# FFN2's operands formed in place from x, held as two half tiles from FFN1's end to FFN2's end

## The chip, the cores and the metric

The kernel runs on one core of a Trainium2 chip. The metric is the device time of one execution in microseconds (us), the median of the runs shown. Five engines work side by side: TensorE (PE), VectorE (DVE), ScalarE (ACT), GpSimd (POOL) and SyncE (SP), each with its own queue of instructions; SP and POOL, and here and there ACT, issue the transfers (DMA).

## The reference

One decoder layer on 1024 prompt tokens and 32 sample tokens (8 sequences of 4), with a width of 1024 and 2816 hidden units:

```python
h = _modulate(_rms(x, p["ffn1_norm"]), sh1, sc1)
x = x + 0.5 * g1[:, None, :] * _swiglu(h, p["ffn1_w_gate"], p["ffn1_w_up"], p["ffn1_w_down"])
h = _modulate(_rms(x, p["mix_norm"]), sh2, sc2)
m, new = _mixer(h, conv[l], hst[l], shift[l], wkv[l], p)
x = x + g2[:, None, :] * m
h = _modulate(_rms(x, p["ffn2_norm"]), sh3, sc3)
x = x + 0.5 * g3[:, None, :] * _swiglu(h, p["ffn2_w_gate"], p["ffn2_w_up"], p["ffn2_w_down"])
y = _rms(x, final_norm)
```

`_swiglu` is `(silu(h @ w_gate) * (h @ w_up)) @ w_down`. The mixer projects h, runs a gated linear recurrence (RG-LRU) on one half of the channels and a matrix-state recurrence (RWKV-7, here in 16 chunks of 64 tokens) on the other, and projects back with `w_out`. Shifts, scales and gates come from the conditioning input; the states of the samples are inputs and outputs.

## The kernel before

x is kept transposed: 128 partitions hold 8 blocks (k) of the 1024 channels, each with its tokens side by side, 1056 and 4 of padding (XW = 1060). The stages follow one another: FFN1 up, FFN1 down, mixer, FFN2 up, FFN2 down with the final norm.

Every matrix product runs as three passes (`mm3`, L61 to L63) over high and low parts. `split` makes the two parts of a weight or an operand: a copy on ACT (L46, tiles wh, fh) and a subtraction on DVE (L47, tiles wl, fl).

An FFN's up stage (`up_phase`) pairs token columns 0 to 527 (pair 0) with 528 to 1055 (pair 1). The hidden units come in 22 blocks; blocks 0 and 1 are plain products (tiles pg, pu), the others use fewer products of summed weights and summed operands (tiles pX, pY, pZ, pW, operands b and t1 to t4). For that `pair_rstd` makes the norm's factor of a pair (squares nt, sums nps by a matmul, factor rn, spread over the partitions as npb and nrs), `pair_unit` (L236) multiplies x by it, `Blocks.split` (L275, L276) makes the operands b and b2, `pair_scale` (L240) scales, and `sums` and `split_sums` make t1 to t4. In FFN2 the pairs are read from DRAM (dX, L1353) into tiles of their own, after the end of the mixer has stored x there (L1316).

The down stage (`down`) loads hidden rows back from DRAM (dh, L489), splits them, multiplies by the down weights into PSUM tiles pd, which rotate over seven buffers (`F`), and `acc_x` (L463, L466) adds each pd to x on DVE, the samples' part to sacc. The mixer's `w_out` does the same with tiles po. Its last part (`w_out_end`) is the third token piece (tokens 768 on) of the first half of the channels, in two output groups (og).

x is one tile. In FFN1 down it is loaded from the input by three transfers (L1481), in FFN2 down by four from dX (L1316). In between, the parts of x that lie in DRAM are scratch for the mixer (`Lg`, `LRO`). Pools (`opened`) place tiles in on-chip memory; a tile waits for those that held its place. The order of instructions on an engine is the scheduler's, by priorities and its own estimates of time, except under `in_order`, where it is the program's. Small constants of the recurrence (tiles spt, L578 to L592) are computed on DVE beside FFN1 down.

## Time and profile before

| what | value |
|---|---|
| median of 3 runs | 2209.8 us (2209.15 to 2214.6) |
| the profiled execution | 2204.8 us, span 2203.0 us |
| mean granted TensorE clock | 0.977 |
| PE / DVE / ACT / POOL busy | 95% / 64% / 34% / 10% |
| stages, by the timeline | FFN1 up to 562, FFN1 down to about 830, mixer to 1437, FFN2 up to 1922, FFN2 down to the end |

A row of the timeline gives the start and the length in us, the engine, the line, the operation, the tiles (output, then inputs), the shapes and how many instructions were put together; square brackets give the engine's idle time ahead of it and what ended that. In a table of windows, each engine has its busy us and in parentheses its instructions; PEclk is the share of full speed that TensorE's clock was granted.

### The profile page before, as it was taken

How to read it: one execution, taken by the hardware profiler on the slowest of the kernel's cores; microseconds unless marked ns; L12 is line 12 of the kernel's file. 1: busy time of each engine (PE TensorE's matmuls, PEld its weight loads, DVE VectorE, ACT ScalarE, POOL GpSimd, SP SyncE). 2: the span in 40 equal slices, each digit the busy share in tenths (PEclk: the TensorE clock that was granted, in tenths of full speed). 3: DMA queues.
4: the chain of work that ended last, by engine and by line, in shares of the span. 5: the costliest groups of instructions: out<-in, count | busy, mean ns of one | idle time of the engine just before them, and what ended most of it. 6: DMA issues, size and time to landing. Idle time of an engine off the chain costs nothing.

```text
span 2203.0 us, 41916 instructions
## 1 busy us (share of the span) xinstructions
PE 2098.9 (95%) x17209; PEld 1989.5 (90%) x17209; DVE 1409.2 (64%) x2954; ACT 743.2 (34%) x1289; POOL 209.4 (10%) x310
## 2 busy tenths in 40 slices
PE   6899999999999999999998899879999999999997
PEld 4899999999999998898886689879999999999997
DVE  5855555565865565775855775687666666585655
ACT  5633232333311135443342441264333333331213
...
PEclk8999999999999999999998999889999999999998
...
GB/s 253 88 152 144 140 148 140 136 148 90 251 107 73 84 67 65 87 117 163 122 177 157 190 173 143 140 125 69 83 75 77 83 79 73 123 205 74 109 37 79
DMA packets 148414, 266.80 MB, mean 121 GB/s; under 512 B 76272, under 2 KB 92800, under 8 KB 146176
## 3 DMA queue, kind: packets, MB, share of 16 engines
...
q8 instruction: 135, 2.21, 0.4%
q14 instruction: 55, 0.45, 0.1%
...
## 4 chain that ended last, share of the span: by engine, by line
PE 76%; DVE 10%; DMA 3%; issue 3%; ACT 3%; POOL 1%; SPq 1%; ACTq 0%; DVEq 0%; POOLq 0%
PE pd L61 7%; PE pd L62 7%; PE pd L63 7%; PE pX L61 4%; PE pZ L61 4%; PE pX L62 4%; PE pZ L63 4%; PE pX L63 4%; PE pW L61 4%; PE pW L63 4%; PE pW L62 4%; PE pZ L62 4%; PE pY L63 2%; PE pY L61 2%; PE pY L62 2%
## 5 line engine op out<-in xcount | busy, mean ns | idle before, releaser
L61 PE MATMUL pd<-fl,wh 128*128 128x384 f32 (+1 forms) x1056 | 340.9, 326 | 3.5 <-DVE fl L47 2.6
L63 PE MATMUL pd<-fh,wh 128*128 128x384 f32 (+1 forms) x1056 | 341.4, 324 | 0.0
L62 PE MATMUL pd<-fh,wl 128*128 128x384 f32 (+1 forms) x1056 | 341.4, 324 | 0.0
L46 ACT ACTIVATE wh<-wr 128x512 fp32r<-128x512 f32 (+1 forms) x254 | 192.1, 761 | 254.5 <-PE pZ L63 71.7
L47 DVE TENSOR_TENSOR wl<-wr,wh 128x512 fp32r<-128x512 f32 (+1 forms) x254 | 215.0, 851 | 89.8 <-ACT wh L46 84.3
L61 PEld LDWEIGHTS pd<-fl,wh 128*128 128x128 f32 x1056 | 198.9, 189 | 5.2 <-ACT wh L46 2.7
L62 PEld LDWEIGHTS pd<-fh,wl 128*128 128x128 f32 x1056 | 199.7, 189 | 0.0
L63 PEld LDWEIGHTS pd<-fh,wh 128*128 128x128 f32 x1056 | 199.4, 189 | 0.0
L61 PE MATMUL pW<-t,wh 128*128 128x266 f32 (+1 forms) x640 | 182.6, 285 | 0.0
L63 PE MATMUL pW<-t,wh 128*128 128x266 f32 (+1 forms) x640 | 182.3, 285 | 0.0
L62 PE MATMUL pW<-t,wl 128*128 128x266 f32 (+1 forms) x640 | 182.2, 285 | 0.0
L463 DVE SCALAR_TENSOR_TENSOR x<-pd,g3c,x 128x384 f32<-128x384 f32 (+1 forms) x192 | 107.0, 568 | 83.1 <-PE pd L63 83.1
L463 DVE SCALAR_TENSOR_TENSOR x<-pd,g1c,x 128x384 f32<-128x384 f32 (+1 forms) x192 | 107.4, 567 | 76.7 <-PE pd L63 76.6
L419 ACT ACTIVATE e<-e,bt 128x262 f32<-128x262 f32 x80 | 41.3, 516 | 293.8 <-DVE bt L418 274.2
L344 POOL DMA_DIRECT2D dh<-hf x88 | 48.0, 545 | 972.4 <-DVE hf L425 793.9
L46 ACT ACTIVATE fh<-wr 128x1056 fp32r<-128x1056 f32 x44 | 47.5, 1082 | 243.2 <-PE pd L63 193.7
L62 PEld LDWEIGHTS pW<-t,wl 128*128 128x128 f32 x640 | 120.8, 189 | 0.0
L61 PEld LDWEIGHTS pW<-t,wh 128*128 128x128 f32 x640 | 120.5, 188 | 0.0
L63 PEld LDWEIGHTS pW<-t,wh 128*128 128x128 f32 x640 | 120.5, 188 | 0.0
L47 DVE TENSOR_TENSOR wl<-s,wh 128x512 fp32r<-128x512 f32 x120 | 82.6, 689 | 55.3 <-ACT wh L46 55.2
L416 DVE TENSOR_TENSOR e<-pZ,e 128x266 f32<-128x266 f32 x80 | 34.4, 430 | 104.3 <-PE pZ L63 104.1
L46 ACT ACTIVATE wh<-s 128x512 fp32r<-128x512 f32 x120 | 75.4, 629 | 65.9 <-PE pW L63 31.4
(495 smaller groups left out, 5888.8 us busy)
## 6 DMA issues: line engine op xcount, KB each, us to landing
wa<-in_w_ada SPq DMA_DIRECT2D x72, 512.0 KB, 3.9
dh<-hf POOLq DMA_DIRECT2D x88, 264.0 KB, 2.3
...
wr<-in_ffn_w_gate SPq DMA_DIRECT2D x44, 512.0 KB, 3.5
wr<-in_ffn_w_up SPq DMA_DIRECT2D x44, 512.0 KB, 3.5
wr<-in_ffn_w_down SPq DMA_DIRECT2D x44, 512.0 KB, 4.2
ch<-dc ACTq DMA_DIRECT2D x32, 512.0 KB, 6.5
wr<-in_w_in SPq DMA_DIRECT2D x22, 512.0 KB, 3.9
```

Source lines behind the costliest of these rows:

```text
L46: nc.scalar.activation(hi, raw, AF.Copy)
L47: nc.vector.tensor_tensor(lo, raw, hi.bitcast(F32), op=ALU.subtract)
L61: nc.tensor.matmul(ps, wh, xl, start=(first and i == 0), stop=False, **kw)
L62: nc.tensor.matmul(ps, wl, xh, start=False, stop=False, **kw)
L63: nc.tensor.matmul(ps, wh, xh, start=False, stop=(last and i == n - 1), **kw)
L344: nc.gpsimd.dma_start(self.dH[m][:, 528 * p:528 * p + 528], hf)
L416: tt(g2, pz, u, op=ALU.add)
L419: nc.scalar.activation(g2[:, 0:n], g2[:, 0:n], AF.Silu, bias=bt[:, 0:1])
L463: nc.vector.scalar_tensor_tensor(x[:, ob, c:c + np_], ps[:, 0:np_], g[:, ob, 0:1], x[:, ob, c:c + np_], op0=ALU.mult, op1=ALU.add)
```

## The change

x becomes two tiles x0 and x1 (class `Halves`) of four channel blocks each, 4256 elements wide per partition (HW), in a pool that lives until the end. The second FFN's operands are views into them (`pair`): pair 0's and pair 1's loads into tiles of their own go, x is still stored to dX for the last addition, and a half's tile is allocated anew after FFN2 up (`x.new`) and read back from dX. The space of x0 serves as t2 and t4 of pair 0 (`t24`) once x0 has been used up, so x0 is read back later than x1. Every transfer, clearing and addition of x over all blocks becomes one per half (`HK`).

`w_out_end` goes; its place is taken by a block in which pair 0's norm factor and its eight `pair_unit` are made between the first product of output group 0 and the rest. In that block the raw weight tiles become three (one before) and the split ones three (four before). The mixer's scratch moves: the recurrence's (A to D) into x1, `Lg`'s six slots become three in each half, the samples' and the first gated output's into x0. In FFN2 up the pools are laid out anew, pair 1's norm sums start two blocks earlier in block 1, and a pool `gap` moves the hidden rows of FFN2 down's first groups to another place.

```diff
@@ -23,6 +23,7 @@
 
 XW = T + 4
 PAIRS = ((0, 264), (528, 266))
+HW = 4256
 SHC, NSH = T, T - (528 + 266)
 NORM_EPS = 1e-6
 GROUPS = [(0, 2), (2, 4)] + [(g, g + 3) for g in range(4, 22, 3)]
@@ -131,8 +132,30 @@
     eps = const.tile([128, 1], F32, name="eps")
     nc.vector.memset(eps, NORM_EPS)
 
+
+    class Halves:
+        def __init__(self, pool):
+            self.pool = pool
+            self.new()
+
+        def new(self):
+            self.t = [self.pool.tile([128, HW], F32, tag=f"x{i}", name=f"x{i}") for i in range(2)]
+            self.v = [t[:, 0:KD // 2 * XW].rearrange("p (k t) -> p k t", k=KD // 2) for t in self.t]
+
+        def __getitem__(self, at):
+            _, k, c = at
+            if isinstance(k, slice):
+                i = k.start // 4
+                return self.v[i][:, k.start - 4 * i:k.stop - 4 * i, c]
+            return self.v[k // 4][:, k % 4, c]
+
+
+        def pair(self, p, i):
+            return self.v[i][:, :, 528 * p:528 * p + 2 * PAIRS[p][1]].rearrange("p k (j t) -> p j k t", j=2)
+
+    HK = [slice(0, 4), slice(4, 8)]
     x = None
-    LRO = {"A": 4 * XW - 32, "B": 5 * XW, "C": 6 * XW, "D": 7 * XW}
+    LRO = {"A": 0, "B": 1084, "C": 2140, "D": 3196}
     mod = const.tile([128, 72, 9], F32, name="mod")
 
 
@@ -293,10 +319,13 @@
             for o, a, b in ((r(0, 0), r(0, 1), r(0, 0)), (r(0, 1), r(1, 1), r(0, 1)), (r(1, 1), r(1, 1), r(0, 0)), (r(1, 0), r(1, 0), r(1, 1))):
                 adder.tensor_tensor(o, a, b, op=ALU.subtract)
 
+
         def split_sums(self, tags):
-            for tag, (o, i, j) in zip(tags, (("t2", 1, 1), ("t1", 0, 0), ("t3", 0, 1), ("t4", 1, 0))):
+            for n, (o, i, j) in enumerate((("t1", 0, 0), ("t3", 0, 1), ("t2", 1, 1), ("t4", 1, 0))):
                 src = self.q(i, j)
-                self.o[o] = h, l = self.both(tag, o)
+                if n == len(tags) == 2:
+                    t = xp.tile([128, HW], F32R, tag="x0", name="t24")
+                self.o[o] = h, l = self.both(tags[n], o) if n < len(tags) else self.parts(t[:, 2128 * (n - 2):2128 * (n - 1)])
                 split(src, h, l)
 
     class Up:
...
@@ -1027,7 +1057,7 @@
             for p in range(2):
                 nc.tensor.transpose(pt[:, c, p].rearrange("p a t -> p (a t)"), yc[:, 4 * c + 2 * p:4 * c + 2 * p + 2].rearrange("p a b -> p (a b)"), ident)
         if "y" not in m:
-            gated(t0, 2 * CL, lambda j: pt[:, :, j // 2, j % 2, :], lambda sh, dt, n: x[:, 0:4, t0:t0 + 2 * CL] if n == "o1" else o(sh, dt, n), "q")
+            gated(t0, 2 * CL, lambda j: pt[:, :, j // 2, j % 2, :], lambda sh, dt, n: x[:, HK[0], t0:t0 + 2 * CL] if n == "o1" else o(sh, dt, n), "q")
             return
         o1 = gated(t0, 2 * CL, lambda j: pt[:, :, j // 2, j % 2, :], o, "q")
         ci = t0 // 384
@@ -1304,16 +1325,17 @@
     g1c = const.tile([128, KD, 9], F32, name="g1c")
     g3c = const.tile([128, KD, 9], F32, name="g3c")
     g2c = mod[:, 40:48, :]
-    rn3 = const.tile([128, 6], F32, name="rn3")
+    xp = None
     dX = [dram.tile([128, KD, 528], F32, name=f"dx{p}") for p in range(2)]
 
 
     def dx_move(queue, c, n, store, k0=0, k1=KD):
         for p in range(2):
             b, e = max(c, 528 * p), min(c + n, 528 * p + 528)
-            if e > b:
-                s, d = x[:, k0:k1, b:e], dX[p][:, k0:k1, b - 528 * p:e - 528 * p]
-                queue.dma_start(*((d, s) if store else (s, d)))
+            for h in HK:
+                if e > b and k0 < h.stop and h.start < k1:
+                    s, d = x[:, h, b:e], dX[p][:, h, b - 528 * p:e - 528 * p]
+                    queue.dma_start(*((d, s) if store else (s, d)))
 
     def norm_pool(ph):
         return opened(ph, "sp", {"t": 3, "sq": 2, "acc": 1, "rs": 2, "adar": 1, "rn": 2, "bt": 3}, side="right")
...
@@ -1344,13 +1367,16 @@
 
             def load_x(p):
                 w = PAIRS[p][1]
+                if rest is None:
+                    X[p] = [x.pair(p, i) for i in range(2)]
+                    return
                 X[p] = [slot(f"x{p}{i}", F32, f"x{p}{i}")[:, 0:8 * w].rearrange("p (j k t) -> p j k t", j=2, k=4) for i in range(2)]
                 for i in range(2):
                     for j in range(2):
                         n = min(w, 528 - w * j)
                         if n < w:
                             nc.gpsimd.memset(X[p][i][:, j, :, n:w], 0.0)
-                        (nc.sync if rest else nc.gpsimd).dma_start(X[p][i][:, j, :, 0:n], xsrc[p][:, 4 * i:4 * i + 4, w * j:w * j + n])
+                        nc.sync.dma_start(X[p][i][:, j, :, 0:n], xsrc[p][:, 4 * i:4 * i + 4, w * j:w * j + n])
 
             sn = [0, None]
 
@@ -1373,9 +1399,8 @@
                         for rs0 in r0:
                             pass
                     else:
-                        rs0 = spread(rn3, WU, spr)
                         W0 = up.plain(*R0)
-                    for k in range(KD):
+                    for k in range(KD) if rest else ():
                         pair_unit(X[0], 0, k, rs0)
                 if first:
                     first(sp, stage)
@@ -1398,9 +1423,9 @@
                     for k in range(KD):
                         next(late, None)
                         ps = up.plain_mm(W1, B[0], 0, k, k + 1, ps)
-                        if k == 1:
+                        if k == (1 if rest else 0):
                             next(r1)
-                        if k == 3:
+                        if k == (3 if rest else 1):
                             rs1 = next(r1)
                     for _ in late:
                         pass
@@ -1425,11 +1450,12 @@
                             up.plain_mm(W, B[1], 1, 0, KD, ps, js=(1,))
                         up.plain_out(u, ps, kept[:, T * u:T * u + T])
             B[1].sums(nc.vector)
-            B[1].split_sums(("e0", "e1", "c1", "x10"))
+            B[1].split_sums(("e1", "c1", "e0", "x10" if rest else "x00"))
         W = up.summed(*raws.pop(0))
         B[0].sums(nc.vector)
-        B[0].split_sums(("x11", "e2", "c0", "x00"))
-        wa = slot("x01", F32, "wa")
+        B[0].split_sums(("e2", "c0", "x11", "x00") if rest else ("e2", "c0"))
+        if rest:
+            wa = slot("x01", F32, "wa")
         bg = rest(sp, lambda k: wa[:, 1024 * (k % 2):1024 * (k % 2) + 1024]) if rest else iter(())
         with in_order(nc.tensor):
             for u in range(2, NH):
@@ -1469,8 +1495,8 @@
                  ("a10", "e0", "e1", "x10", "a11", "a12", "c1", "x01", "a00", "x11", "e2", "c0", "a01", "a02", "x00"), (), (),
                  first, lambda sp, stage: ada8(0, PY, sp, stage), rest)
     hp = None
-    xt = mx.enter_context(tc.tile_pool(name="xp", bufs=1, reuse_waits="tile")).tile([128, KD * XW], F32, tag="x", name="x")
-    x = xt.rearrange("p (k t) -> p k t", k=KD)
+    xp = es.enter_context(tc.tile_pool(name="xp", bufs=1, reuse_waits="tile"))
+    x = Halves(xp)
     with ExitStack() as ph:
         hid = opened(ph, "hid", {"fh": 3, "fl": 3}, side="right")
         sp = norm_pool(ph)
...
@@ -1478,7 +1504,8 @@
         early = ph.enter_context(ExitStack())
         more = Rows(early, "hidB", ("fh", "fl", "wh", "wl"), 3)
         for c, n in CH[::-1]:
-            nc.gpsimd.dma_start(x[:, :, c:c + n], xT[:, :, c:c + n])
+            for h in HK:
+                nc.gpsimd.dma_start(x[:, h, c:c + n], xT[:, h, c:c + n])
 
 
         def main_done():
@@ -1524,9 +1551,10 @@
 
         def Lg(name, n=T):
             ln[0] += 1
-            return xt[:, 1080 * (ln[0] % 6):1080 * (ln[0] % 6) + n]
-        wa = xt[:, 6480:6480 + T]
-        m["w2"] = xt[:, 7552:7552 + 512]
+            o = 1056 * (ln[0] % 3)
+            return x.t[ln[0] // 3 % 2][:, o:o + n]
+        wa = x.t[0][:, 3192:3192 + T]
+        m["w2"] = x.t[1][:, 3192:3192 + 512]
         nc.sync.dma_start(m["w2"], a["w2a2"])
         first = [Shifted(12), Shifted(4)]
         for j, *p in head:
...
@@ -1646,25 +1674,40 @@
         nc.sync.dma_start(a["hO"], m["hO"])
 
     with ExitStack() as ph:
-        PL_["w"] = PL_["wr"] = opened(ph, "wC", {"wr": 1, "wh": 4, "wl": 4})
-        tmp = opened(ph, "rC", {"nt": 1})
-        r3 = pair_rstd(0, lambda k: x[:, k, 0:528].rearrange("p (j t) -> p j t", j=2), lambda sh, name: P.tile(sh, F32, tag="wu", name=name),
-                       type("R", (), {"tile": staticmethod(lambda sh, dt, tag, name: rn3)}), tmp.tile([128, 2128], F32, "nt", "nt"))
-        for _ in range(2):
-            next(r3)
-        w_out_end()
+        PL_["w"] = PL_["wr"] = opened(ph, "wC", {"wr": 3, "wh": 3, "wl": 3})
+        nt = ph.enter_context(tc.tile_pool(name="rC", bufs=1, reuse_waits="tile")).tile([128, 2128], F32, tag="nt", name="nt")
+        rn = PL_["mc"].tile([128, 6], F32, name="rn3")
+        own = type("R", (), {"tile": staticmethod(lambda sh, dt, tag, name: rn if tag == "rn" else nt[:, 528:1056])})
+        W = [w_load(0, og) for og in range(2)]
+        r3 = pair_rstd(0, lambda k: x.pair(0, k // 4)[:, :, k % 4], lambda sh, name: P.tile(sh, F32, tag="wu", name=name), own, nt)
+        next(r3)
+        w0 = w_block(W[0], 0, 0, 2)
+        next(w0)
+        next(r3)
+        next(w0)
+        rs = next(r3)
+        for k in range(KD):
+            pair_unit([x.pair(0, i) for i in range(2)], 0, k, rs)
+        for w in (w0, w_block(W[1], 0, 1, 2)):
+            for _ in w:
+                pass
+        add_samples(g2c)
+        for i in range(2):
+            nc.gpsimd.memset(x.v[i][:, :, T:XW], 0.0)
+        dx_move(nc.gpsimd, 768, 288, True)
     mx.close()
     PL_["wn"] = T
     with ExitStack() as ph:
-        up_phase(ph, "ffn2", dX, sc3, 6, ("x10", "x11", "e2", "c1", "x00", "x01", "a10"), ("e0", "e1", "a11", "a12"), ("a00", "c0", "a01", "a02"))
+        up_phase(ph, "ffn2", None, sc3, 6, ("a00", "c0", "a01", "a02", "e2"), (), ("a10", "c1", "a11", "a12", "e0", "e1", "x00"))
+    x.new()
     PL_["wr"] = opened(es, "wrp", {"wr": 3}, side="right")
-    xt = es.enter_context(tc.tile_pool(name="xp", bufs=1, reuse_waits="tile")).tile([128, KD * XW], F32, tag="x", name="x")
-    x = xt.rearrange("p (k t) -> p k t", k=KD)
     with ExitStack() as ph:
         hid = opened(ph, "hid", {"fh": 3, "fl": 3}, side="right")
         sp = norm_pool(ph)
         PL_["w"] = opened(ph, "wp", {"wh": 3, "wl": 3}, side="right")
         early = ph.enter_context(ExitStack())
+
+        early.enter_context(tc.tile_pool(name="gap", bufs=1, reuse_waits="tile")).tile([128, 11000], F32, name="gap")
         more = Rows(early, "hidB", ("fh", "fl", "wh", "wl"), 3)
         for c, n in CH[::-1]:
             dx_move(nc.gpsimd, c, n, False)
```

The change moves instructions. In the rows below x_6357 is x0 and x_6358 is x1 of the first allocation, x_21289 and x_21290 those of the second; x_15572 is the tile of its own that pair 0 had before. Line numbers are those of each kernel (L492 is the add of `acc_x`, before L463; L48 the subtraction of `split`, before L47; L260 `pair_unit`, before L236).

DVE at the end of w_out, before:

```order
L463 SCALAR_TENSOR_TENSOR x<-po,mod,x 128x256
L466 TENSOR_TENSOR sacc<-po,sacc 128x32
L245 TENSOR_TENSOR shd<-mod 128x64
L472 TENSOR_TENSOR sacc<-sacc,mod 128x256
L473 TENSOR_TENSOR x<-x,sacc 128x8x32
L476 MEMSET sacc 128x256
L47 TENSOR_TENSOR wl<-wr,wh 128x512 x4
L236 TENSOR_TENSOR x_15572<-x_15572,nrs 128x2x264 x4
L276 SCALAR_TENSOR_TENSOR b_15631<-x_15572,sc_94,b_15631 128x264
```

and after:

```order
L48 TENSOR_TENSOR wl<-wr,wh 128x512 x2
L492 SCALAR_TENSOR_TENSOR x_6357<-po,mod,x_6357 128x256
L495 TENSOR_TENSOR sacc<-po,sacc 128x32
L260 TENSOR_TENSOR x_6357<-x_6357,nt 128x528 x4
L260 TENSOR_TENSOR x_6358<-x_6358,nt 128x528 x4
L492 SCALAR_TENSOR_TENSOR x_6357<-po,mod,x_6357 128x256
L495 TENSOR_TENSOR sacc<-po,sacc 128x32
L48 TENSOR_TENSOR wl<-wr,wh 128x1024
```

The splits of FFN2's first weights and the eight multiplications of pair 0 stood behind the last addition of w_out; now they stand ahead of the last five.

DVE at the start of FFN1 down, before:

```order
L463 SCALAR_TENSOR_TENSOR x<-pd,g1c,x 128x256
L466 TENSOR_TENSOR sacc<-pd,sacc 128x32
L463 SCALAR_TENSOR_TENSOR x<-pd,g1c,x 128x256
L466 TENSOR_TENSOR sacc<-pd,sacc 128x32
L581 TENSOR_TENSOR spt_8411<-spt_8410 128x4
L463 SCALAR_TENSOR_TENSOR x<-pd,g1c,x 128x384
L584 TENSOR_TENSOR spt_8412<-spt_8412,spt_8411 128x4
L463 SCALAR_TENSOR_TENSOR x<-pd,g1c,x 128x384
L585 TENSOR_SCALAR spt_8412<-spt_8412 128x4
```

and after:

```order
L614 TENSOR_TENSOR spt_8415<-spt_8415,spt_8414 128x4
L615 TENSOR_SCALAR spt_8415<-spt_8415 128x4
L616 TENSOR_TENSOR spt_8415<-spt_8415,spt_8413 128x4
L618 SCALAR_TENSOR_TENSOR spt_8416<-spt_8415,spt_8416 128x4
L621 TENSOR_SCALAR sp2c<-spt_8416 128x4
L622 TENSOR_SCALAR nsp_8448<-spt_8416 128x4
L492 SCALAR_TENSOR_TENSOR x_6357<-pd,g1c,x_6357 128x256
L495 TENSOR_TENSOR sacc<-pd,sacc 128x32
L492 SCALAR_TENSOR_TENSOR x_6357<-pd,g1c,x_6357 128x256
```

The small steps on spt stood between the additions, one at a time; now two additions (blocks 3 and 7) are followed by 19 of these steps in a row, of which the last six are shown, and then by the other additions.

POOL in FFN2, from the last store of hidden rows on, before:

```order
L344 DMA dh<-hf 128x528 x43
L1316 DMA x<-dx_99 128x8x288
L1316 DMA x<-dx_98 128x8x144
L1316 DMA x<-dx_99 128x8x240
L1316 DMA x<-dx_98 128x8x384
L344 DMA dh<-hf 128x528
```

and after:

```order
L373 DMA dh<-hf 128x528 x38
L1338 DMA x_21289<-dx_98 128x4x288
L373 DMA dh<-hf 128x528
L1338 DMA x_21289<-dx_97 128x4x144
L1338 DMA x_21289<-dx_98 128x4x240
L1338 DMA x_21289<-dx_97 128x4x384
```

Here only x0's four loads are left; x1's stand 38 stores earlier. The last store of hidden rows now stands behind one of x0's loads and ahead of three.

35 lines of the change are left out of this document (16 added, 19 removed).

## The prediction

> **What bounds the kernel now.** I began with the busy shares, the slices and the shares of the chain that ended last.
>
> ```profile
> PE 2098.9 (95%) x17209; PEld 1989.5 (90%) x17209; DVE 1409.2 (64%) x2954; ACT 743.2 (34%) x1289; POOL 209.4 (10%) x310
> PE   6899999999999999999998899879999999999997
> PEclk8999999999999999999998999889999999999998
> PE 76%; DVE 10%; DMA 3%; issue 3%; ACT 3%; POOL 1%; SPq 1%; ACTq 0%; DVEq 0%; POOLq 0%
> ```
>
> TensorE (PE) is the bound nearly everywhere; only its idle time and its half-clock time can be gained, and each new stall of it is lost in full. So the windows come next.
>
> ```profile
> 500.00:700.00 200.00, 200.00 (x1365) 198.83 (x1364) 131.79 (x287) 51.24 (x67) 5.95 (x9) 1.00 0.40 133
> 1000.00:1300.00 300.00, 276.31 (x3128) 237.37 (x3124) 195.64 (x453) 120.00 (x200) 63.34 (x99) 0.94 0.68 163
> 1430.00:1440.00 10.00, 7.67 (x60) 7.44 (x58) 5.70 (x18) 2.86 (x6) 0.49 (x1) 0.99 0.43 157
> 1440.00:1450.00 10.00, 5.12 (x23) 5.12 (x24) 10.00 (x20) 7.40 (x15) 3.46 (x7) 0.50 0.89 287
> 1460.00:1470.00 10.00, 6.27 (x45) 6.09 (x44) 6.12 (x11) 2.21 (x4) 0.00 (x0) 0.85 0.00 0
> 1470.00:1480.00 10.00, 8.78 (x70) 8.41 (x68) 7.47 (x19) 6.38 (x16) 0.00 (x0) 0.98 0.01 2
> 1480.00:1490.00 10.00, 8.06 (x57) 7.47 (x58) 8.99 (x26) 8.94 (x24) 0.00 (x0) 1.00 0.00 0
> 1490.00:1500.00 10.00, 6.83 (x56) 6.61 (x55) 10.00 (x14) 7.89 (x13) 0.00 (x0) 1.00 0.03 13
> 1900.00:2000.00 100.00, 96.55 (x630) 94.90 (x629) 66.15 (x130) 23.99 (x27) 5.20 (x7) 0.98 0.54 175
> ```
>
> The columns are the length, the busy us and counts of PE, PEld, DVE, ACT and POOL, then the granted clock. FFN1's passage from up to down (500 to 700) has no idle PE at all. Three places that the change touches have some: the end of w_out and the start of FFN2 (1430 to 1500, 2.33 + 4.88 + 10.06 us, and half clock in one window), FFN2's passage to down (3.45), and the mixer (23.7 in 1000 to 1300). What ends the idle stretches:
>
> ```profile
> 1435.89 0.49 DVE L463 SCALAR_TENSOR_TENSOR x<-po,mod,x 128x256 f32<-128x256 f32 x1 [1.02 <-PE po L63]
> 1437.71 0.48 DVE L463 SCALAR_TENSOR_TENSOR x<-po,mod,x 128x256 f32<-128x256 f32 x1 [1.24 <-PE po L63]
> 1439.52 2.42 DVE L47 TENSOR_TENSOR wl<-wr,wh 128x512 fp32r<-128x512 f32 x4
> 1441.87 2.56 DVE L236 TENSOR_TENSOR x<-x,nrs 128x528 f32<-128x528 f32 x4
> 1444.88 0.59 PE L61 MATMUL pg<-b,wh 128*128 128x264 f32 x1 [7.21 <-DVE b L276]
> 1446.18 0.77 POOL L1353 DMA_DIRECT2D x<-dx  x1 [5.81 <-ACT b L275]
> 1446.93 0.14 POOL L1352 MEMSET x<- 128x16 f32 x1
> 1465.75 1.07 PE L210 MATMUL nps<-ones,nt 128*88 128x1 f32 x12 [3.73 <-DVE nt L206]
> 1480.68 0.39 PE L61 MATMUL pg<-b,wh 128*128 128x266 f32 x1 [1.09 <-DVE b L276]
> 1482.77 4.24 ACT L240 ACTIVATE x<-x,sc 128x266 f32<-128x266 f32 x10
> 1499.26 0.39 PE L61 MATMUL pu<-b,wh 128*128 128x266 f32 x1 [3.17 <-ACT e L380]
> 1499.49 0.28 PE L62 MATMUL pu<-b,wl 128*128 128x266 f32 x1
> 1499.61 0.28 PE L63 MATMUL pu<-b,wh 128*128 128x266 f32 x1
> 1510.10 0.29 PE L61 MATMUL pX<-b,wh 128*128 128x266 f32 x1
> ```
>
> After the last add (1437.71) DVE splits unit 0's weights and scales pair 0 while PE stands 7.21 us; the loads of pair 1 are issued only at 1446, so its norm sums reach PE 3.73 us late; 3.17 us are lost to the gate's exponent on ACT. The first regular product starts at 1510.10.
>
> **The start of FFN2, in four terms.** (1) Unit 0's weight splits (2.42 us) and the eight scalings of pair 0 (2.56 for four, 5.12 in all) now stand in DVE's order before w_out's last adds; what remains between last product and unit 0 is the start of the splits of x, about 1.5 us by my count of the rows. But in w_out DVE then makes no add for 5.12 + 1.22 (one weight split of 128x1024, twice a 128x512 one: 2.42 / 4 x 2) = 6.3 us, and the PSUM tiles that PE may still fill cover some 2.3 of these (one add per 1.8 us, from 1435.89 to 1437.71, is PE's own rate here, and I count between one and two free tiles): a new stall of 4. Gain 7.21 - 1.5 - 4 = 1.7; ends -0.6 (nothing covered) and +5.7 (all covered). (2) At 1444.88 the gap is followed by half clock, so 5.12 busy us of that window did 2.56 us of work. The new gaps are shorter; I take half of it, 1.3, between 0 and 2.6. (3) Of the 10.06 idle us in 1460 to 1500 the wait for pair 1's loads goes, since no load is left, and its norm is taken a step earlier; the small waits for splits go with it. The exponent's stall stays and grows: ACT's ten scalings of 4.24 us now stand later, and some six of them (2.5) come ahead of it, 3.17 + 2.5 = 5.7. Gain 4.4, ends 0 and 6.9. (4) The clock of 0.85 in 1460 to 1470 becomes full: 0.15 x 6.27 = 0.9. Sum -8.3, ends +0.6 and -16. Pair 0's own loads lay beside w_out and save nothing more. At nothing I cost the memset (0.14 on POOL, once a half, and POOL waited 5.81 us ahead of its loads there), the samples' add in two halves (DVE is idle 4.3 us in 1430 to 1440) and the three raw weight tiles of w_out (their loads are ahead of their splits even now); without that cover they cost their own length, under 1 us together.
>
> **FFN1 up to down.** This term speaks against the change, and nothing in the change's purpose shows it.
>
> ```profile
> 548.22 2.67 POOL L1481 DMA_DIRECT2D x<-in_xT  x3 [9.22 <-ACT e L421]
> 563.02 0.47 DVE L463 SCALAR_TENSOR_TENSOR x<-pd,g1c,x 128x256 f32<-128x256 f32 x1
> 572.50 0.16 DVE L585 TENSOR_SCALAR spt<-spt 128x4 f32<-128x4 f32 x1
> 572.69 0.16 DVE L584 TENSOR_TENSOR spt<-spt,spt 128x4 f32<-128x4 f32 x1
> 1932.11 0.34 PE L61 MATMUL pd<-fl,wh 128*128 128x384 f32 x1
> 1932.28 0.34 PE L62 MATMUL pd<-fh,wl 128*128 128x384 f32 x1
> ```
>
> Before, three loads of x go out together, and each add waits for its own columns. A half tile is 4256 wide, no multiple of the 1060 of a block, so a load or add over several blocks counts as touching all between: the program's waits make the loads of one half follow each other's landing, and make every add to x0 but the fourth block's wait for all three. The order around it has turned: after the adds of blocks 3 and 7 stand 19 small steps of the mixer's constants (spt, each on the one before), and only then the next add. At 0.19 us (572.50 to 572.69) these are 3.6 us without an add. The first add starts at 563.02 as before; six spt steps (1.1) follow, and the second add, whose tile I put at 565.2, ends near 565.9. The third then starts at 569.5 and ends near 570.2 (0.47 and the samples' 0.2). PE has one tile left to fill (six matmuls of 0.17: 1.0 us, to 566.9) and stands 3.3 us. Three later waits in the same group, behind DVE's splits of the next group's operands, I count at 0.7 + 0.7 + 0.8. Sum +5.5. Nothing gives it back, as PE was never idle here. Ends: 0 (the PSUM tiles cover it) and +9 (half clock behind it too).
>
> **FFN2 up to down.**
>
> ```profile
> dh<-hf POOLq DMA_DIRECT2D x88, 264.0 KB, 2.3
> 1905.51 0.33 SPq L489 DMA_DIRECT2D wr<-dh  x1
> 1916.43 3.54 POOL L1316 DMA_DIRECT2D x<-dx  x4 [3.00 <-PE pZ L63]
> 1924.15 1.77 PE L61 MATMUL pd<-fl,wh 128*128 128x288 f32 x7 [2.56 <-DVE fl L47]
> 1925.72 0.44 PE L62 MATMUL pd<-fh,wl 128*128 128x288 f32 x1
> 1928.02 0.29 PE L62 MATMUL pd<-fh,wl 128*128 128x288 f32 x1
> ```
>
> Before, the hidden rows are loaded at 1905 and their split ends PE's wait of 2.56; then matmuls start 0.24 apart until 1928 instead of 0.13, which loses another 1.8; the rest of the 3.45 idle us is 0.9. Now the gap pool puts these rows where room comes free about a unit earlier, and a group of five matmuls moves even among the last products: 2.56 + 1.8 + 0.9 = 5.3 can go. Against it, x0 can be loaded only after PE's last reading of t24 (near 1922), in three steps, each behind the landing of the one before (2.5 to 3 us by the row at 1916.43, about 0.9 to issue, and 2.3 us to landing in the stores' row): complete near 1932, while x1 came long before. Four adds to x1 cover the first steps; then an add to x0 stands behind three splits, and I count PE waits of 2.0 + 0.6 + 0.9 = 3.5, with clock loss 0.8. Net -1.0; ends -5.3 and +3.
>
> **The mixer.** The recurrence's scratch now shares x1, the gated output and the sample's scratch share x0; counts of instructions are the same. Its loads of x from DRAM are eight, as before. I take 0, from -3 to the third rival's price.
>
> **Sum.** The profiled execution is 2204.8 us, 1.8 of them outside the span of 2203.0, and 5.0 under the median of 2209.8 of the runs shown. -8.3 + 5.5 - 1.0 + 0 = -3.8: 2201.0 on the profile's scale, 2206 as a median. 0.3% of 2209.8 is 6.6 us, about what a measurement can tell from no change.
>
> **Rivals.** First, the stalls are covered. If PSUM's tiles carry PE over the spt steps (0) and over the scalings (5.7), and the other terms reach their good ends (2.6 + 6.9 + 0.9, and 3.6 at FFN2's passage), it is -19.7: 2190. For it speaks that 64% DVE leaves room; against it the counted free tiles.
>
> Second, PE's clock falls after each new gap. At 1924.15 a gap of 2.56 us was followed by 3.7 us of matmuls at half speed, a loss of 1.8. Such a loss after the stall in w_out, at the exponent, and in FFN1's passage is 5.5, and term (2) loses its 1.3: -3.8 + 6.8 = +3, so 2213. Against it: after 3.17 us at 1499.26 the second matmul follows 0.23 later and the third 0.12 after that, which is full speed.
>
> [...]
>
> Third, slower: the mixer.
>
> ```profile
> ch<-dc ACTq DMA_DIRECT2D x32, 512.0 KB, 6.5
> ```
>
> Its chain is a series of sixteen chunk steps (two loads of ch each), and in 1000 to 1300 PE idles 23.7 us in it. Gated output and sample scratch now share x0, and four-block writes to it count as overlapping. A wait of 1 us in each step is +16: +12 in all, 2222. It decides from 10.4 / 16 = 0.65 us a step, the point at which the sum passes +6.6. For it speaks that waits there are on the chain; against it, that I found the same producers ahead of most of its steps.
>
> **How the numbers follow.** Forecast (2200 to 2210) 0.45, first rival 0.17, second 0.22, third 0.16. Faster by over 0.3% means under 2203.2: the first rival and half of the forecast's case, 0.40. Slower is over 2216.4: the third rival and a little of the second, 0.18. Within: 0.42. The range leaves out the far end of the first rival and most of the third: 2191 to 2218.
>
> **What would show it.** Right: no load of pair 1 and no 3.73 wait before nps; unit 0 within 2 us of w_out's last product, but a gap of about 4 inside w_out ended by a DVE add; a PE gap of about 3 near 566 ended by an add that follows spt steps; first pX near 1502 less the shift of the earlier stall; the wait before FFN2's first pd gone, and one ended by an x0 add near 1932. Wrong: 500 to 700 without idle PE, or windows of 1000 to 1300 that differ from 276 busy us by more than 5.

## The result, and the profile after

The changed kernel took 2227.2 us (median of four executions, 2225.4 to 2232.5), the kernel before 2210.8 on the same chip (median of four). The ratio is 1.0075, 95% interval 1.0055 to 1.0095: slower, and above the range's 2218. The profiled execution is 2225.4 us, its span 2223.6, 20.6 more than before. The profile of the kernel before lies 6.0 us under its median and that of after 1.8 under, so some 4 of these 20.6 us are scatter between executions.

The page of after, its busy shares and the shares of the chain that ended last ("issue", 3% before, is time for which the profile shows no wait; it is not followed here):

```profile
PE 2117.3 (95%) x17209; PEld 2006.3 (90%) x17209; DVE 1412.7 (64%) x2958; ACT 743.5 (33%) x1291; POOL 212.7 (10%) x317
PE 59%; issue 18%; DVE 10%; DMA 4%; ACT 4%; POOL 1%; SPq 1%; ACTq 0%; DVEq 0%; POOLq 0%
```

The number of products is the same, so the 18.4 us more of busy PE are slower products. The granted clock (0.972 in the mean, 0.977 before) is some 11 us of the span; part of the rest is that the first product behind a stall is listed longer (0.37 to 0.45 us in the rows near 570 below, where the prediction's rows have 0.29 to 0.34). The two windows by which the prediction was to be judged, of after:

```profile
500.00:700.00 200.00, 194.69 (x1332) 191.67 (x1330) 130.61 (x285) 50.91 (x67) 8.34 (x13) 0.99 0.42 137
1000.00:1300.00 300.00, 279.65 (x3144) 241.26 (x3143) 191.07 (x439) 114.72 (x186) 64.41 (x99) 0.94 0.68 157
```

500 to 700 has its idle PE (5.31 us), and 1000 to 1300 is within 3.4 us of before's 276.31: neither sign of a wrong theory. Next the execution in six stretches, bounded by the same products in both kernels: from FFN1's first pd to the first nps of the mixer's norm, to the first za of the mixer, to the start of the last four ptY, to FFN2's first pX, to its last pX, to the last pd. Columns as in the prediction's windows; first the kernel before:

```profile
554.65:793.30 238.65, 238.65 (x1484) 238.46 (x1483) 153.06 (x318) 50.76 (x55) 8.60 (x9) 1.00 0.35 114
793.30:860.22 66.92, 58.34 (x356) 56.20 (x356) 49.81 (x121) 32.61 (x61) 22.63 (x25) 0.95 0.32 98
860.22:1401.84 541.62, 510.90 (x5365) 449.38 (x5365) 359.95 (x811) 200.62 (x332) 94.22 (x142) 0.96 0.58 142
1401.84:1510.10 108.26, 88.40 (x637) 86.50 (x637) 82.63 (x169) 59.06 (x115) 5.08 (x9) 0.89 0.33 114
1510.10:1918.39 408.29, 408.29 (x3337) 408.29 (x3336) 258.12 (x529) 134.76 (x258) 24.16 (x44) 1.00 0.23 79
1918.39:2184.65 266.26, 262.81 (x1635) 261.14 (x1634) 165.38 (x315) 61.93 (x78) 16.41 (x17) 0.99 0.33 106
```

and after:

```profile
558.60:805.28 246.68, 241.38 (x1484) 239.99 (x1483) 155.31 (x318) 50.46 (x55) 10.76 (x12) 0.99 0.35 111
805.28:877.64 72.36, 61.89 (x368) 59.75 (x367) 51.03 (x123) 34.75 (x64) 24.48 (x28) 0.93 0.27 79
877.64:1421.33 543.69, 513.77 (x5355) 452.56 (x5354) 359.92 (x811) 199.56 (x330) 93.14 (x141) 0.96 0.59 143
1421.33:1521.98 100.65, 89.04 (x637) 87.50 (x637) 75.45 (x163) 58.15 (x113) 2.83 (x6) 0.90 0.22 74
1521.98:1935.86 413.88, 410.90 (x3338) 410.68 (x3336) 268.27 (x540) 138.72 (x262) 25.29 (x45) 1.00 0.26 88
1935.86:2205.47 269.61, 264.09 (x1635) 262.70 (x1633) 162.86 (x311) 58.52 (x75) 17.83 (x19) 0.98 0.27 89
```

The differences are +8.0, +5.4, +2.1, -7.6, +5.6 and +3.3 us; with +4.0 ahead of FFN1's first pX (100.38 to 104.36) they make 20.8. Only the fourth is a gain. What ended PE's new idle stretches in after, and POOL's loads of x:

```profile
568.30 0.37 PE L62 MATMUL pd<-fl,wh 128*128 128x288 f32 x1 [1.02 <-DVE spt L611]
570.10 0.41 PE L62 MATMUL pd<-fl,wh 128*128 128x384 f32 x1 [0.77 <-DVE spt L615]
574.04 0.45 PE L62 MATMUL pd<-fl,wh 128*128 128x384 f32 x1 [2.64 <-DVE sacc L495]
580.60 0.44 PE L62 MATMUL pd<-fl,wh 128*128 128x384 f32 x1 [0.55 <-DVE x L492]
582.26 0.44 PE L62 MATMUL pd<-fl,wh 128*128 128x384 f32 x1 [0.33 <-DVE sacc L495]
1454.61 0.37 PE L62 MATMUL po<-h2ly,wh 128*128 128x288 f32 x1 [2.73 <-DVE sacc L495]
1462.10 0.39 PE L62 MATMUL pg<-b,wh 128*128 128x264 f32 x1 [1.21 <-DVE b L302]
1509.61 0.39 PE L62 MATMUL pu<-b,wh 128*128 128x266 f32 x1 [3.48 <-ACT e L409]
1537.00 0.42 PE L62 MATMUL pY<-t,wh 128*128 128x264 f32 x1 [2.98 <-DVE t L48]
1951.77 0.44 PE L62 MATMUL pd<-fl,wh 128*128 128x384 f32 x1 [1.80 <-DVE x L492]
1953.80 0.69 PE L62 MATMUL pd<-fl,wh 128*128 128x384 f32 x1 [0.71 <-DVE x L492]
1959.00 0.69 PE L62 MATMUL pd<-fl,wh 128*128 128x384 f32 x1 [2.91 <-DVE sacc L495]
...
552.14 1.50 POOL L1508 DMA_DIRECT2D x<-in_xT  x2 [6.69 <-ACT fh L47]
557.64 0.75 POOL L1508 DMA_DIRECT2D x<-in_xT  x1 [1.15 <-DMA x<-in_xT]
562.10 0.75 POOL L1508 DMA_DIRECT2D x<-in_xT  x1 [3.71 <-DMA x<-in_xT]
1940.01 0.76 POOL L1338 DMA_DIRECT2D x<-dx  x1 [6.21 <-PE pW L64]
1945.12 1.52 POOL L1338 DMA_DIRECT2D x<-dx  x2 [3.57 <-DMA x<-dx]
1951.49 0.75 POOL L1338 DMA_DIRECT2D x<-dx  x1 [4.86 <-issue]
```

FFN1's passage: 5.31 us of stalls, and 2.7 of slower products behind them (8.0 - 5.3), of which 1.7 are half clock (granted 0.50 from 574.7 to 578.1, 1.00 behind it). Its loads of x wait for the landing of one another, where before all three left together at 548.22. FFN2's start: as foretold, the 7.21 ahead of unit 0 is 1.21, a stall of 2.73 stands in w_out, the exponent's wait is 3.48. At 1537 a wait that the prediction did not have: the first pY of pair 0 waits for a split of its sums, whose first in-place subtraction (at 1523.73) stands behind pair 1's last split from x (1520.61). FFN2's passage: x0's loads go out at 1940, 1945 and 1951, each behind the landing of one before.

### The profile page after: what moved, and what is told of

Its sections match the earlier page's. It is cut to its first block, busy times and chain, and to the rows that moved or that the text cites. A ratio compares the mean times of both kernels' runs of the same rounds, so it can differ in the third digit from the quotient of the medians.

```text
span 2223.6 us, 41931 instructions
## 1 busy us (share of the span) xinstructions
PE 2117.3 (95%) x17209; PEld 2006.3 (90%) x17209; DVE 1412.7 (64%) x2958; ACT 743.5 (33%) x1291; POOL 212.7 (10%) x317
## 4 chain that ended last, share of the span: by engine, by line
PE 59%; issue 18%; DVE 10%; DMA 4%; ACT 4%; POOL 1%; SPq 1%; ACTq 0%; DVEq 0%; POOLq 0%
PE pd L62 7%; PE pd L63 7%; PE pd L64 7%; PE pX L62 2%; PE pZ L62 2%; PE pZ L64 2%; PE pZ L63 2%; PE pX L64 2%; PE pX L63 2%; PE pW L62 2%; PE pW L63 2%; PE pW L64 2%; PE adaps L169 2%; PE po L62 1%; PE po L64 1%
## 5 line engine op out<-in xcount | busy, mean ns | idle before, releaser
L62 PE MATMUL pd<-fl,wh 128*128 128x384 f32 (+1 forms) x1056 | 345.4, 327 | 10.8 <-DVE sacc L495 5.9
L47 ACT ACTIVATE wh<-wr 128x512 fp32r<-128x512 f32 (+1 forms) x254 | 192.1, 761 | 249.2 <-DMA wr<-in_ffn_w_down 72.4
L48 DVE TENSOR_TENSOR wl<-wr,wh 128x512 fp32r<-128x512 f32 (+1 forms) x254 | 215.0, 851 | 83.5 <-ACT wh L47 80.6
L492 DVE SCALAR_TENSOR_TENSOR x<-pd,g3c,x 128x384 f32<-128x384 f32 (+1 forms) x192 | 107.8, 569 | 95.5 <-PE pd L64 90.3
L492 DVE SCALAR_TENSOR_TENSOR x<-pd,g1c,x 128x384 f32<-128x384 f32 (+1 forms) x192 | 107.1, 568 | 80.0 <-PE pd L64 79.7
L47 ACT ACTIVATE fh<-wr 128x1056 fp32r<-128x1056 f32 x44 | 47.3, 1082 | 264.4 <-PE pd L64 232.9
L48 DVE TENSOR_TENSOR wl<-s,wh 128x512 fp32r<-128x512 f32 x120 | 82.6, 689 | 57.0 <-ACT wh L47 57.0
L47 ACT ACTIVATE wh<-s 128x512 fp32r<-128x512 f32 x120 | 75.4, 629 | 66.3 <-PE pW L64 31.0
```

The source lines that it names most:

```text
L47: nc.scalar.activation(hi, raw, AF.Copy)
L48: nc.vector.tensor_tensor(lo, raw, hi.bitcast(F32), op=ALU.subtract)
L62: nc.tensor.matmul(ps, wh, xl, start=(first and i == 0), stop=False, **kw)
L492: nc.vector.scalar_tensor_tensor(x[:, ob, c:c + np_], ps[:, 0:np_], g[:, ob, 0:1], x[:, ob, c:c + np_], op0=ALU.mult, op1=ALU.add)
```

## The experiments

All stretches in us, worked out from each profile at the same bounds (the rows above are the first two lines). "Start" is the time of FFN1's first pX; "ratio" is to the kernel before on the same chip, with its 95% interval. The runs were spread over several chips, where the kernel before took 2210.2 to 2212.6, so kernels are compared by the ratio.

| kernel | start | FFN1 down | its end | mixer | to FFN2's pX | FFN2 up | FFN2 down | median | ratio |
|---|---|---|---|---|---|---|---|---|---|
| before | 100.4 | 238.6 | 66.9 | 541.6 | 108.3 | 408.3 | 266.3 | 2210.8 | |
| after | 104.4 | 246.7 | 72.4 | 543.7 | 100.7 | 413.9 | 269.6 | 2227.2 | 1.0075 (1.0055-1.0095) |
| e1 | 101.7 | 238.5 | 70.1 | 562.3 | 105.2 | 409.1 | 259.8 | 2221.0 | 1.0039 (1.0026-1.0052) |
| e2 | 103.0 | 253.2 | 73.0 | 555.5 | 107.5 | 408.3 | 278.5 | 2254.2 | 1.0185 (1.0167-1.0202) |
| e3 | 102.9 | 247.2 | 72.2 | 543.0 | 101.5 | 413.8 | 269.5 | 2228.6 | 1.0075 (1.0059-1.0091) |
| e4 | 103.3 | 246.5 | 74.7 | 543.0 | 101.4 | 413.8 | 269.3 | 2226.6 | 1.0064 (1.0051-1.0078) |
| e5 | 101.6 | 246.8 | 74.4 | 545.9 | 101.8 | 413.8 | 260.0 | 2217.9 | 1.0038 (1.0024-1.0052) |
| e6 | 103.4 | 238.6 | 70.5 | 547.1 | 101.4 | 415.3 | 260.0 | 2212.7 | 1.0008 (0.9997-1.0019) |
| e7 | 101.4 | 238.5 | 72.8 | 563.1 | 103.4 | 409.1 | 259.9 | 2217.5 | 1.0032 (1.0017-1.0046) |
| e8 | 102.5 | 238.6 | 72.1 | 547.3 | 101.1 | 409.1 | 259.8 | 2203.7 | 0.9962 (0.9949-0.9976) |
| e9 | 104.2 | 247.2 | 72.1 | 546.1 | 101.8 | 413.8 | 269.5 | 2228.2 | 1.0063 (1.0043-1.0082) |
| e10 | 104.2 | 238.6 | 72.1 | 550.4 | 101.4 | 409.1 | 265.1 | 2203.7 | 0.9953 (0.9929-0.9978) |
| e11 | 103.0 | 238.6 | 68.8 | 549.8 | 101.1 | 409.1 | 259.8 | 2209.2 | 0.9992 (0.9976-1.0007) |

**e1, blocks that fill the tile.**

```diff
-XW = T + 4
+XW = T + 8
```

> One number is changed in the changed kernel: a block of x is 1064 elements wide instead of 1060, so that four blocks fill a half tile of 4256 exactly. Layout, pools, scratch and the order in the program stay. My theory: with 1060 an access over several blocks counts as touching all that lies between, and these false waits make most of the 20.6 us. Then x's loads no longer follow one another, the adds of FFN1's first group come in the order of the blocks with a spt step between two of them, and pair 0's sums stand ahead of the reading of pair 1. In numbers: in FFN1's passage the stalls of 1.02 + 0.77 + 2.64 us near 570 shrink to under 1 in all and the passage loses under 2 us instead of 8.1; the wait of 2.98 us ahead of the first pY of pair 0 near 1537 and the half clock behind it go (5.6 us); FFN2's passage loses 0 to 2 us instead of 3.3. Sum -12 to -16 against the changed kernel: 2211 to 2215 on the median's scale, which is the kernel before within 0.3%. Rival, that the layout in two half tiles costs it (shared scratch, pools, the additions by halves): 2227 within 3 us, with the same stalls. Rival, that the nineteen spt steps alone matter: -5 to -8, with the wait near 1537 unchanged.

The three places came out as my theory has it: FFN1 down 238.5 with no idle PE, FFN2 up 409.1, FFN2 down 259.8 instead of 269.6. The loads of x go out in one burst again:

```profile
549.49 3.72 POOL L1508 DMA_DIRECT2D x<-in_xT  x5 [6.69 <-ACT fh L47]
```

The total missed its 2211 to 2215, because the mixer took 562.3 us, 18.6 more than in after. That this one number moved 8.2 + 4.8 + 9.8 us, with the waits gone from the traces, shows that the false waits cause these three losses; e5 tests the third by itself, e6 the first. What it does to the mixer is another matter (e7).

**e2, the reverse: the kernel before with a tile a little too wide** (at both places where x is allocated).

```diff
-...tile([128, KD * XW], F32, tag="x", name="x")
-    x = xt.rearrange("p (k t) -> p k t", k=KD)
+...tile([128, KD * XW + 32], F32, tag="x", name="x")
+    x = xt[:, 0:KD * XW].rearrange("p (k t) -> p k t", k=KD)
```

> The kernel before, with only this changed: the tile of x is 32 elements wider per partition than its eight blocks of 1060, so that, as in the changed kernel's half tiles, blocks do not fill the tile. Nothing moves in memory but what lies behind x; operands still go through DRAM. My theory, that such views are tracked as whole stretches: x's three loads in FFN1 down come one behind the other, the first adds wait for all of them, some twenty spt steps stand in a row ahead of the first add, and PE, which had no idle time in 500 to 700, stands 4 to 10 us there; with the loads of x in FFN2 down the whole is 6 to 14 us slower than before (2217 to 2225). Rival, that half tiles, scratch or pools cost it: no change, 2211 within 3 us, and no idle PE in 500 to 700.

Thirty-two unused elements cost 41 us, with no half tile, no shared scratch and no other pool; I had expected 6 to 14. FFN1's passage and down are 14.6 longer, FFN2's 12.2, and the mixer 13.9 and FFN1's end 6.1, which I had not expected and did not trace. The profile shows the same chain as in after, longer still (POOL's loads, the first add, PE):

```profile
550.85 0.91 POOL L1481 DMA_DIRECT2D x<-in_xT  x1 [9.22 <-ACT fh L46]
558.41 0.90 POOL L1481 DMA_DIRECT2D x<-in_xT  x1 [3.28 <-DMA x<-in_xT]
569.31 0.90 POOL L1481 DMA_DIRECT2D x<-in_xT  x1 [1.00 <-DMA x<-in_xT]
578.18 0.48 DVE L463 SCALAR_TENSOR_TENSOR x<-pd,g1c,x 128x256 f32<-128x256 f32 x1 [0.35 <-DMA x<-in_xT]
578.91 0.58 PE L61 MATMUL pd<-fl,wh 128*128 128x288 f32 x1 [12.06 <-DVE sacc L466]
```

FFN2's start and up, where x is not used in place, stay (107.5 and 408.3). So such views are enough for losses of this kind in both down stages; the rival, that only the new layout can cause them, falls.

**e3, the spt steps on GpSimd.**

```diff
...
-            nc.vector.tensor_tensor(t[3], t[3], t[2], op=ALU.mult)
-            nc.vector.tensor_scalar(t[3], t[3], 1.0 / d, None, op0=ALU.add)
+            nc.gpsimd.tensor_tensor(t[3], t[3], t[2], op=ALU.mult)
+            nc.gpsimd.tensor_scalar(t[3], t[3], 1.0 / d, None, op0=ALU.add)
...
```

> The changed kernel with the 22 small steps of the series in spt on GpSimd instead of VectorE; the order of the adds and the false waits for x's loads stay. If the spt steps between the adds are what makes PE stand near 570, then 3 to 5 of the 5.3 us of stalls there go, and with them some of the half clock: -4 to -8, 2219 to 2223. If the adds to x0 themselves come late, because they wait for three loads one behind the other, the stalls stay, ended by an add and not by spt: 2227 within 2. The start of FFN2 and its passage to down stay as they are in either case.

No change: 2228.6, and FFN1 down 247.2. VectorE now stands instead of stepping, and PE's later stall is 3.01 us in place of 2.64 + 0.55 + 0.33. But VectorE stands for two things: an add for x0's last load, and then, in its order ahead of the next adds, a step of the series (L618) for GpSimd's slower ones (0.20 to 0.22 us each and some 0.30 apart, against 0.16 to 0.17 and 0.20 apart on VectorE in after):

```profile
569.41 0.48 DVE L492 SCALAR_TENSOR_TENSOR x<-pd,g1c,x 128x256 f32<-128x256 f32 x1 [0.93 <-DMA x<-in_xT]
574.23 0.16 DVE L618 SCALAR_TENSOR_TENSOR spt<-spt,spt 128x4 f32<-128x4 f32 x1 [2.73 <-POOL spt L616]
577.54 0.69 PE L62 MATMUL pd<-fl,wh 128*128 128x384 f32 x1 [3.01 <-DVE x L492]
```

So the run moved the steps without taking them off the path, and does not separate them from the loads. A row of after does so in part, x0's last load, issued at 562.10:

```profile
x<-in_xT POOLq DMA_DIRECT2D x1, 768.0 KB, 8.9
```

It landed near 571.0, and the adds went on at 573.41, behind spt steps without a gap: of the 3.5 us without an add from 569.95 on, the load accounts for about 1.0 and the steps for 2.4. In e1 and e6 VectorE makes the same steps between the adds, and PE never waits: only with the false waits do they stand in a row.

**e4, scalings written behind w_out.**

```diff
-        for k in range(KD):
-            pair_unit([x.pair(0, i) for i in range(2)], 0, k, rs)
         for w in (w0, w_block(W[1], 0, 1, 2)):
             for _ in w:
                 pass
+        for k in range(KD):
+            pair_unit([x.pair(0, i) for i in range(2)], 0, k, rs)
```

> The changed kernel with the eight scalings of pair 0 written behind w_out's last adds instead of between its two output groups; all else stays in place. It tests the first term of my prediction (scalings in w_out cost a stall of 4 us there, 2.73 measured, and take 7.21 us of waiting away ahead of unit 0). By the term: the stall of 2.73 us in w_out goes and a wait of 6 to 8 us comes back ahead of the first pg, ended by a split of b, with half clock behind it: +3 to +7, 2230 to 2234. Rival, that the scalings are hidden in either place: within 2 of 2227.

The experiment failed as one: the scheduler put VectorE's and ScalarE's instructions where they were. It is a second measurement of the changed kernel, and it tells how far a stretch repeats: within 0.8 us, but for the end of FFN1 (74.7 against 72.4) and the start. The mixer scatters more: e5 and e9, with VectorE's order of after there, have 545.9 and 546.1 against 543.7 and 543.0. e9 asks the question again.

**e5, exact blocks only where FFN2 down adds.** The second pair of x tiles gets blocks of 1064 (`x.w = 1064` ahead of `x.new()`); the first keeps 1060.

> The changed kernel, with blocks of 1064 only in the second pair of x tiles, those that FFN2 down reads back from DRAM and adds to; the first pair, from FFN1's end to FFN2's, keeps 1060, and all up to FFN2's last products keeps its order. It separates FFN2's passage from all else. My theory: between the last pX and the last pd the time falls by what the run with 1064 everywhere gained there (it lost 3.3 us against the kernel before with 1060 and gained 6.4 with 1064): -9 to -10, about 2217. Rival, that the passage gained there because the mixer ahead had another order: 2227 within 2.

Hit: 2217.9, FFN2 down 260.0 with PE never idle. The four late loads leave together:

```profile
1942.68 2.99 POOL L1338 DMA_DIRECT2D x<-dx  x4 [6.20 <-PE pW L64]
```

The 9.6 us are 5.5 of idle PE and 4.1 of slower products (the granted clock of after was 0.50 from 1953.7 to 1963.9).

**e6, the false waits taken away with blocks of 1060 in the first pair of x tiles.** On e5:

```diff
-        for c, n in CH[::-1]:
-            for h in HK:
-                nc.gpsimd.dma_start(x[:, h, c:c + n], xT[:, h, c:c + n])
+        for k in range(KD):
+            nc.gpsimd.dma_start(x[:, k, 0:T], xT[:, k, 0:T])
...
             B[1].sums(nc.vector)
+            if rest is None:
+                B[0].sums(nc.vector)
             B[1].split_sums(...)
```

(and `B[0].sums` no longer stands behind it in FFN2).

> As the run before it in this list, with two more changes that take false waits away and leave the blocks at 1060: x's loads in FFN1 down are one transfer for each block over all tokens (eight instead of six), which touches nothing between blocks, and pair 0's sums stand in the program ahead of pair 1's splits instead of behind them. By my theory FFN1's passage loses under 1.5 us instead of 8.1, the wait of 2.98 us ahead of pair 0's first pY and its half clock go (5.6), FFN2's passage gains 9 to 10, and the mixer, whose order stays near the changed kernel's, keeps its loss of 5 to 8: 2227 - 8 - 5.6 - 9.7 = 2204, between 2200 and 2208, faster than the kernel before. If the mixer's time hangs on its order by chance, it can lose up to 20 more, as the run with 1064 did. If eight loads on GpSimd come too late for the adds, PE stands near 565 again and the whole is 2210 to 2214.

FFN1 down is 238.6 with PE never idle, so its 8 us come from the loads' false waits, by a second way. But pair 0's four subtractions of 1.25 us now stand between pair 1's splits, and a wait of 4.65 us comes ahead of pair 1's first pY: FFN2 up 415.3, no gain. Hence 2212.7 instead of 2204, the kernel before within its interval.

**e7, exact blocks and another mixing.** e1 with `st=3` for `st=2` in the table of the mixer's steps.

> The kernel with blocks of 1064 everywhere, and one number of the mixer changed: the sample's steps are mixed with the other branch's from the third instead of the second on (st 3 for 2). It asks whether the 20 us that the mixer lost with 1064 belong to the layout or to the order in which the scheduler put the mixer's steps. If to the order: another order gives another loss, by more than 3 us either way, 2200 to 2218; FFN1's passage, the first pY of pair 0 and FFN2's passage stay as good as they were with 1064. If to the layout (1064, shared scratch): 2221 within 3.

The ratio is e1's within its interval, and the mixer's stretch is the same (563.1 against 562.3). So I could not show that e1's mixer lost its 20 us by a chance of order: with 1064 it is 562 and 563 in two orders, with 1060 in the first pair between 543 and 550 in the nine other profiles of the changed layout, in three orders of VectorE. The 1064 profiles have 45.1 and 40.3 us of idle PE there, the nine 28.4 to 33.6. Why stays open.

**e8, pair 0 scaled in w_out, its sums where VectorE was idle.** On e6:

```diff
             pair_unit([x.pair(0, i) for i in range(2)], 0, k, rs)
+            pair_scale([x.pair(0, i) for i in range(2)], 0, k, sc3)
...
                     r1 = pair_rstd(1, ...)
                     next(r1)
+                    if rest is None:
+                        B[0].sums(nc.vector)
```

(pair 0's operands are then split from the scaled x, and its scaling behind pair 1's goes).

> The run with block loads, with pair 0's sums moved once more: pair 0 is also scaled in place on ScalarE while w_out still runs (its operands are then split from the scaled x), and its sums stand on VectorE right behind pair 1's squares, where it was idle for some 4 us near 1470, instead of ahead of pair 1's splits. In the run before, that place cost 4.8 us between the first pX and the first pY of pair 0 and 2.2 later. My theory: both go, and the wait for the gate's exponent (3.48 us) shrinks, since ScalarE's eight scalings of pair 0 no longer stand around it: -6 to -9 against the block-load run's 2212.7, 2204 to 2207, 0.15 to 0.3% under the kernel before. Rival, that DVE's 5 us of sums near 1470 only move the wait to pair 1's norm (nrs, then pg): a new wait of 3 to 5 us ahead of pair 1's first pg, and -2 at most.

2203.7 us, faster than both kernels: 0.38% less than the kernel before (0.24 to 0.51), where the changed kernel takes 0.75% more. FFN2 up is 409.1 with PE never idle. The exponent's wait did not shrink (4.13 us); pair 1's first pg waits 0.93, not 3 to 5. The profile does not show the gain in sum: its span is 2203.0, that of the kernel before, whose profile lies 6.0 under its median. So losses of a few us against that one profile, FFN1's end and the mixer above all, may be scatter.

**e9, scalings held behind w_out.** e4's text, with VectorE held to the program's order there (`with in_order(nc.vector)`).

> The changed kernel, with VectorE held to the program's order at the end of w_out, where the eight scalings of pair 0 now stand behind the last adds (in the earlier try the program's text alone moved, and the instructions came out in the same order as before it). By my first term: the stall of 2.73 us in w_out goes (with its half clock, up to 2 more), and the wait ahead of unit 0's first pg grows from 1.21 us by the scalings' 5.1 us: from w_out's last po back to the first pg the kernel is 2 to 4 us slower net, 2229 to 2232. Rival, that the scalings are hidden in either place: 2227 within 1.5. Rival, that half clock behind the stall in w_out costs more than the wait: -1 to -3.

The row of the timeline ahead of unit 0:

```profile
1466.19 0.59 PE L62 MATMUL pg<-b,wh 128*128 128x264 f32 x1 [6.49 <-DVE b L302]
```

The stall of 2.73 in w_out is gone and the wait ahead of unit 0 is 6.49 instead of 1.21, as expected in kind; the exponent's wait is 4.96 instead of 3.48. In sum the stretch is 101.8, against 100.7 to 101.8 in four profiles of the other order: 0 to 1.1 us, where I had expected 2 to 4. The scalings are nearly as well placed behind w_out.

**e10, no gap pool.** e8 without the `gap` tile.

> The run with scalings in w_out, without the pool that moves FFN2 down's first hidden rows to another place; all up to FFN2 up stays in order. It asks what that pool is worth. By my second term of FFN2's passage, the earlier loads of the rows took 5.3 us of waits away: without it PE waits 2 to 3 us again ahead of the first pd for the split of fl, with half clock behind, +4 to +6, 2208 to 2210. Rival, that the wait went because x is no longer loaded by one queue behind pair 0's columns: no change, 2204 within 2.

The profiled execution shows the 5.3 us (265.1 against 259.8), but by another mechanism than mine: no wait for fl ahead of the first pd, but one of the adds for x0's load, and PE behind it:

```profile
1941.66 0.48 DVE L495 SCALAR_TENSOR_TENSOR x<-pd,g3c,x 128x256 f32<-128x256 f32 x1 [2.92 <-DMA x<-dx]
1942.39 0.37 PE L62 MATMUL pd<-fl,wh 128*128 128x288 f32 x1 [3.63 <-DVE sacc L498]
```

With the pool (e8), five pd come ahead of the last pW, and x0's first load lands after 4.3 us instead of 8.1: its adds wait 1.7 us in all, and PE not at all. The timed runs do not show the 5.3: the ratios are 0.9953 and 0.9962, e10's five runs lie between 2198.7 and 2215.3, and the profiled one is the slowest of them. What the pool is worth is not settled.

**e11, x's stores on SP.** e8 with `dx_move(nc.sync, c, n, True)` behind FFN1's adds.

> The run with scalings in w_out, with the stores of x behind FFN1's adds issued on SP instead of GpSimd. In the changed kernel these are two for each piece instead of one, and the chain of waits at FFN1's end goes through them: GpSimd issues a store (0.75 us) between two additions of the norm's squares, and nps waits for these (3.88 us instead of 3.08). If that is where FFN1's end loses 4.5 us up to the first za: -1 to -3 there. If SP's own queue is late with the hidden rows' or weights' loads behind these stores: +2 to +5. The mixer behind it comes out in another order (some 400 of 4044 products of TensorE move), which by the runs so far is worth up to 10 either way, so the stretch up to the first za is read by itself.

FFN1's end is 68.8 instead of 72.1 (70.1 and 70.5 in e1 and e6, with the stores on POOL). The wait ahead of the first nps is 3.88 us in e8 as in after, and shorter in e11 (after and then e11):

```profile
823.91 1.44 PE L209 MATMUL nps<-ones,nacc 128*96 128x1 f32 x8 [3.88 <-POOL nacc L200]
812.02 0.84 PE L209 MATMUL nps<-ones,nacc 128*96 128x1 f32 x8 [1.48 <-POOL nacc L200]
```

The stores that POOL issues between the norm's additions are worth 2.4 us of this wait. In the kernel before, with half as many, it was 3.08, so their doubling accounts for 0.8 of the 5.4 us that FFN1's end lost. The mixer, in another order, took 2.5 more, and the whole came to 2209.2, a ratio of 0.9992 against e8's 0.9962: no gain in sum.

## Why the prediction was wrong, step by step

The sum said -3.8; the profile says +20.8. The 24.6 us between them are FFN2 up (a term missing, 5.6), FFN2 down (a term mis-sized, 4.3), FFN1's end and the mixer, costed at nothing (7.5), FFN1's passage (2.5), FFN2's start (0.7) and the scatter at the kernel's start (4.0).

- **The start of FFN2: right.** -7.6 to the first pX, -8.3 foretold. Inside, errors cancel: the stall in w_out was 2.73 where I put 4, the exponent's 3.48 where I put 5.7, but each has half clock behind it. Moving the scalings by itself is worth 0 to 1.1 (e9) where I put 1.7.
- **FFN1 up to down: the mechanism right, the size short.** +8.0 against +5.5. The idle PE was 5.31, close to the counted 5.5 in part by luck: the stall was 2.64 where I put 3.3, the waits behind it 0.88 where I put 2.2, and I had none ahead of it, where 1.79 stood. The slower products behind it (2.7, of which 1.7 half clock) I had left to the end of the range. The place came out as told, loads one behind the other and then a row of spt steps; the root of both is the false waits, and without these PE does not wait (e1, e6).
- **FFN2 up to down: a mis-sized term.** +3.3 against -1.0. The gain was there (FFN2 down is 6.3 us under before's once the false waits go, e5; I had 5.3). The cost was 9.6, not 4.3. I took x0's steps at 2.5 to 3 us from stores of 264 KB and the issue; the transfers of after have 4.0 to 6.8 us from issue to landing. The kernel before had nearer rows, which I did not use: its own loads of x in FFN2 down, in the view of all its DMA issues (KB each, median us from issue to landing):

```profile
x<-dx POOLq DMA_DIRECT2D x1, 1152.0 KB, 6.6
...
x<-dx POOLq DMA_DIRECT2D x1, 576.0 KB, 8.4
```

- **The step that is missing: pair 0's sums.** I traced the false waits through loads and adds, and not through the in-place sums, which write pair 0's columns while pair 1's are read. 2.98 us of waiting and 1.7 of half clock (granted 0.50 from 1537.2 to 1540.6): e1 and e8 take 4.8 of the +5.6 away. The other 0.8 stays with PE never idle (409.1 in e1, e7, e8, e10 and e11, 408.3 before) and is open.
- **The mixer: nearly right.** From its first za to its last ptY +2.1. That is less than the 3.1 by which it scatters with VectorE's order unchanged, 543.0 to 546.1. But its entry (FFN1's end) lost 5.4, which no term of the sum covered: x's stores there are issued once per half, twice as often, on the engine that also adds the norm's squares. By the wait ahead of the first nps the doubling explains 0.8 (e11). A later nps waits 3.15 instead of 2.13, and the clock was lower (0.93, 0.95 before). What causes these, and how much of the 5.4 is scatter, is open.
- **The start of the kernel: scatter.** +4.0 ahead of FFN1's first pX is no part of the change (last section).
- **The second rival was the better forecast.** It put half clock behind each new gap. I argued against it from one row where full speed followed 3.17 us, and gave it 0.22. In after, every one of the 13 stalls of 2.6 us or more (from 40 us on) had it: the four us behind them were granted 0.50 to 0.66. It still fell 14 us short: of its 2213 it lacks the sums, the true length of the loads, the entry of the mixer and the scatter.

Taken together: of +20.8, false waits are 8.0 + 4.8 + 9.6 = 22.4, the entry and the mixer 7.5, the open rest of FFN2 up 0.8, the scatter at the start 4.0, and the change's own gains are 7.6 and 6.3.
